# Three value projections as half-array pairs into two banks

## The chip, the cores and the metric

The kernel runs on one core of a Trainium2 chip. A core has TensorE for matrix products (PE in the profile, its weight loads PEld), VectorE (DVE) and ScalarE (ACT) for elementwise work, GpSimd (POOL) and SyncE (SP), which here mostly issue DMAs. Products land in PSUM, eight banks of 128 partitions x 512 float32; operands lie in SBUF. The metric is the device time of one execution in microseconds (us).

## The reference

Two decoder layers over 512 tokens of width 1024, float32. Each adds a token mixer and a SwiGLU to the stream, both behind an RMS norm. The second layer's mixer is windowed attention with 16 heads of 64 in three groups; the part that matters is where the values `v` come from and where they go:

```python
def attn_mixer(h, w_qkv, w_out):
    qkv = jnp.einsum('bsd,de->bse', h, w_qkv).reshape(B, S, 3, N_HEADS, HEAD_DIM)
    q = rope(qkv[:, :, 0]) * HEAD_DIM ** -0.5
    k = rope(qkv[:, :, 1])
    v = qkv[:, :, 2]
    for (window, dilation), n_g in zip(ATTN_PATTERNS, HEAD_GROUPS):   # 6, 5, 5 heads
        o_g, lse_g = dilated_window_attention(q[:, :, sl], k[:, :, sl], v[:, :, sl], window, dilation)
        ...
    alpha = jax.nn.softmax(jnp.stack(lses, axis=-1), axis=-1)
    merged = jnp.concatenate([o_g * (N_ATTN_GROUPS * alpha[:, :, g])... for g, o_g in enumerate(outs)], axis=2)
    return jnp.einsum('bse,ed->bsd', merged, w_out)
```

## The kernel before, in words

Every float32 matrix is split into a high and a low part of the type fp32r (`whi` and `wlo` for weights, `h_hi` and `h_lo` for the normed stream), and a product is three: high by high, high by low, low by high (`mm3`, lines 264 to 266). ScalarE makes the high part of a weight tile (CAST, line 171), VectorE the low one (line 175), from a raw tile that a DMA on SyncE's queue loads (line 136). Rings of five raw and five split tiles let this run ahead of TensorE: a load waits until VectorE has made the low part of the tile that lay there, a CAST until TensorE has used the split tile that lay there.

The order on TensorE is written out by hand. The orders on the other engines come from a scheduler, which plays the program through with costs of its own and puts each instruction where it is ready in that play; `tc.high_priority(URGENT)` moves an instruction ahead of others that are ready at the same time. On the chip each engine runs its list strictly in that order.

The attention layer first projects queries and keys, head pair by head pair, with `project`: 8 blocks of the inner dimension x 3 products of 128 x 512 into one bank. `later` puts scores and transposes of earlier heads between the projections; scores (line 1051) and transposes of the softmax numerators `e` (line 1086) work on the two halves of the array, 64 partitions each. Then the values come in two forms:

- The first six heads: `for m in range(3)` calls `project` for two heads at a time. ScalarE copies the bank, reordered, into `vt` (line 1258, tile `ropea`); a projection later `turn` transposes it on TensorE (line 1248), and ScalarE copies that into `v` (line 1249).
- The other ten heads in two parts of five: four banks `pv`, one for each 128 tokens; for each of four weight tiles `c` and each bank `b` six products of 128 x 320 (lines 1272 to 1274).

The banks of these steps come from one pool, `mm`, of four, handed out in turn. Two more pools of two, `psc` and `ptr`, fill the eight. A bank can be written again when the last reader of what it held before is done.

Beside it run `group_sums` and `group_weights` (called by `between` at steps 19 and 21): ScalarE takes the exponential of the heads' maxima `mx` (line 1168), VectorE reduces it into `near` (line 1173), four small DMAs on GpSimd's queue rearrange `near` over partitions into `mx` (line 1176), and VectorE copies that on (COPY, line 1181) and computes the weights of the groups from it (lines 1183 to 1208).

Of the kernel before, what the change touches and what calls it, by code (L numbers as in the profile page):

```python
# [10 lines left out]
F32 = mybir.dt.float32  # L11
# [6 lines left out]
P = 128  # L18
S = 512
D = 1024  # L20
NC = D // P
# [3 lines left out]
HD = 64  # L25
# [5 lines left out]
R = 4  # L31
# [44 lines left out]
def trunk_kernel(ctx: ExitStack, tc: tile.TileContext, x_in, xT, gam, gains, consts, ident_d, w0, wT, w1, wv, w_down, out):  # L76
# [9 lines left out]
    nc = tc.nc  # L86
# [18 lines left out]
    mm = Banks()  # L105
# [16 lines left out]
    def enqueue(src, shape, kind="w", **more):  # L122
        queue.append(dict(kind=kind, src=[src], shape=shape, **more))
        return len(queue) - 1

    def load(i):
        item = queue[i]
        shape = item["shape"]
        n = math.prod(shape)
        raw = (pools["v"] if item["kind"] == "v" else wraw).tile([P, 1024], F32, name="vraw" if item["kind"] == "v" else "wraw")  # L130
        dst = raw[:, :n]
        if len(shape) == 3:
            dst = dst.rearrange("p (g c) -> p g c", g=shape[0])
        elif item.get("rows"):
            dst = dst.rearrange("p (k c) -> p k c", k=shape[0])
        nc.sync.dma_start(dst, item["src"][0])
        for more in item["src"][1:]:
            nc.gpsimd.dma_start(dst, more, accum_op=ALU.add)  # L138
        raws[i] = raw

    def load_sums():

        done = loaded["v"]
        for i in range(len(ready), min(len(queue), len(ready) + 20)):
            if queue[i]["kind"] == "v" and "src" in queue[i] and i not in raws:
                if "v" not in pools or len(done) >= V_TILES and queue[done[-V_TILES]]["last"] >= len(ready):
                    return
                load(i)
                done.append(i)

    def weights(i, split_ahead=4, load_ahead=5, held=0):

        load_ahead = queue[i].get("ahead", load_ahead)
        for n in range(loaded["w"], min(len(queue), i + load_ahead)):
            if queue[n]["kind"] == "w":
                load(n)
            loaded["w"] = n + 1
        load_sums()
        while len(ready) < min(loaded["w"], i + split_ahead):
            item = queue[len(ready)]  # L160
            if item["kind"] == "v" and "v" not in pools:
                break
            if "pool" not in item and len(ready) > i and held + sum("pool" not in it for it in queue[i : len(ready)]) >= RING:
                break
            shape = item["shape"]
            n = math.prod(shape)
            raw = raws[item.get("into", len(ready))]
            hi, lo = (pools.get(item.get("pool"), wspl).tile([P, 1024], F32R, name=item.get("pool", "w") + part) for part in ("hi", "lo"))
            if len(ready):
                with tc.issue_after(item["cast_behind"]) if "cast_behind" in item else nullcontext():  # L170
                    nc.scalar.copy(hi[:, :n], raw[:, :n])  # L171
            else:
                nc.vector.tensor_copy(hi[:, :n], raw[:, :n])
            with tc.issue_after(item["behind"]) if "behind" in item else nullcontext():
                nc.vector.tensor_sub(lo[:, :n], raw[:, :n], hi[:, :n].bitcast(F32))  # L175
            for into, more in item.get("then", ()):
                nc.vector.tensor_add(raws[into][:, :n], raws[into][:, :n], raws[more][:, :n])  # L177
            if "loads" in item:
                into, src = item["loads"]
                nc.gpsimd.dma_start(raws[into][:, :n].rearrange("p (k c) -> p k c", k=shape[0]), src, accum_op=ALU.add)  # L180
            if len(shape) == 2:
                ready.append(tuple(t[:, :n].rearrange("p (k m) -> p k m", k=shape[0]) for t in (hi, lo)))
            else:
                ready.append(tuple(t[:, :n].rearrange("p (g k m) -> p g k m", g=shape[0], k=shape[1]) for t in (hi, lo)))
        got = ready[i]
        ready[i] = None
        return got
# [68 lines left out]
    j_v0 = [enqueue(w0[26 + i], (8, P)) for i in range(3)]  # L256
# [6 lines left out]
    def mm3(ps, whi, wlo, xhi, xlo, first, last, **kw):  # L263
        nc.tensor.matmul(ps, lhsT=whi, rhs=xhi, start=first, stop=False, **kw)  # L264
        nc.tensor.matmul(ps, lhsT=whi, rhs=xlo, start=False, stop=False, **kw)  # L265
        nc.tensor.matmul(ps, lhsT=wlo, rhs=xhi, start=False, stop=last, **kw)  # L266

    def project(j, hi, lo):
        ps = mm.tile([P, S], F32, name="mm")
        whi, wlo = weights(j)  # L270
        for k in range(NC):
            mm3(ps, whi[:, k, :], wlo[:, k, :], hi[:, k, :], lo[:, k, :], k == 0, k == NC - 1)
        return ps


    xs = stat.tile([P, 4 * D], F32, name="x")
    x = xs.rearrange("p (b d) -> p b d", b=4)
# [6 lines left out]
    def tokens_at(shift):  # L284
        both = tokens_both(shift)
        return [both[:, z] for z in range(2)]
# [17 lines left out]
    class Norm:  # L304
# [49 lines left out]
        def turn(self, b, half, tp):  # L354

            for j in range(4):
                at = half * S + j * P
                nc.tensor.transpose(tp[:, j, :], self.tile(b)[:, at : at + P], ident)
# [79 lines left out]
    with ExitStack() as pctx:  # L438
# [12 lines left out]
        h_hi, h_lo = z_hi, z_lo = tokens_at(0)  # L451
# [13 lines left out]
        for c in range(NC):  # L465

            pieces = (slice(0, P), slice(P, S)) if c == 0 else (slice(0, S),)
            if c < 2 or c % 2 == 0:
                if c < 2:
                    load_x(c, pieces[0])  # L470
                whi, wlo = weights(j_in[0][c if c < 2 else 1 + c // 2], 1, 1)
# [7 lines left out]
            k = 0 if c < 2 else c % 2  # L479
# [3 lines left out]
            for b, i in turns:  # L483
                xx, w = parts[i]
                nc.tensor.matmul(  # L485
                    early[b], lhsT=xx[:, c, b * P : (b + 1) * P], rhs=w[:, k, :],
                    start=c == 0 and i == 0, stop=c == NC - 1 and i == 2, skip_group_check=True,
# [15 lines left out]
        v, s, r = (tmp.tile([P, 4], F32, name=name) for name in ("v4", "s4", "r4"))  # L503
# [453 lines left out]
    with ExitStack() as actx:  # L957
# [20 lines left out]
        def blocks_of(a):  # L978

            return a.rearrange("p (r b i) -> p b r i", r=R, b=4)  # L980

        def rope(ps, t, name):
            a = aw.tile([P, S], F32, name="ropea")
            sw = aw.tile([P, S], F32, name="ropeb")
            nc.vector.stream_shuffle(sw, ps, PARTNER)
            nc.vector.tensor_mul(a, ps, cosr)
            nc.gpsimd.tensor_mul(sw, sw, sinr)
            out = aw.tile([P, S], F32, name=name, bufs=3)

            if t >= 3:  # L990
                nc.vector.tensor_add(out, a, sw)
            elif name == "k":
                nc.vector.tensor_add(out.rearrange("p (b r i) -> p b r i", b=4, r=R), blocks_of(a), blocks_of(sw))
            else:
                by_r = lambda z: z.rearrange("p (r j) -> p r j", r=R)
                nc.vector.tensor_add(out.rearrange("p (j r) -> p r j", r=R), by_r(a), by_r(sw))
            return out
# [116 lines left out]
        h_hi, h_lo = tokens_at(0)  # L1114
# [26 lines left out]
        for t in range(8):  # L1141
# [4 lines left out]
            k = rope(pk, t, "k")  # L1146
            later(2 * t + 1)
            if t in (4, 6):
                first = (t, q, k)
# [80 lines left out]
        def between(step, copied=None):  # L1230
            later(step)
            if step == 19:
                group_sums()
            if step == 21:
                group_weights()
            if step == 23:
                with tc.issue_after(copied.ins):
                    spread_weights()
# [11 lines left out]

        step = 16
        for m in range(3):
            ps = project(j_v0[m], h_hi, h_lo)
            if to_turn:
                turn()
            vt = aw.tile([P, S], F32, name="ropea")
            with tc.high_priority(URGENT):
                nc.scalar.copy(vt.rearrange("p (b r i) -> p b r i", b=4, r=R), blocks_of(ps))
            to_turn.append((m, vt))
            between(step)  # L1260
            step += 1
        for part in range(2):
            at = VA + part * VB
            pv = [mm.tile([P, S], F32, name="mm") for _ in range(4)]
            for c in range(4):
                whi, wlo = weights(j_v[part][c])
# [23 lines left out]
        two = mp.tile([P, D], F32, name="even_rows")  # L1290
# [110 lines left out]
```

## Time and profile before

| | us |
|---|---|
| median of three runs | 980.57 (980.44 to 980.94) |
| profiled execution | 981.05 |
| its span, first to last instruction | 979.3 |
| TensorE busy | 971.8 |
| VectorE busy | 784.1 |
| ScalarE busy | 575.9 |
| first of the three projections begins (in the span) | 542.54 |
| last of the three ends, transposes begin | 562.51 |

A row of a timeline gives the start in us from the span's beginning, the duration, engine, line, operation, output<-inputs, shape, how many, and in brackets how long the engine had been idle and who ended that. TensorE's products overlap: a product of 512 columns is listed with 0.39 us, but the next one starts 0.23 us behind it, so the cost of one is read from starts. A row of the windows view has the stretch, its length, busy time and count of PE, PEld, DVE, ACT and POOL, the clock that TensorE was granted (1.00 is full), the DMA engines' busy share, and GB/s.

### The profile page before, as it was taken

How to read it: one execution, taken by the hardware profiler on the slowest of the kernel's cores; microseconds unless marked ns; L12 is line 12 of the kernel's file. 1: busy time of each engine (PE TensorE's matmuls, PEld its weight loads, DVE VectorE, ACT ScalarE, POOL GpSimd, SP SyncE). 2: the span in 40 equal slices, each digit the busy share in tenths (PEclk: the TensorE clock that was granted, in tenths of full speed). 3: DMA queues.
4: the chain of work that ended last, by engine and by line, in shares of the span. 5: the costliest groups of instructions: out<-in, count | busy, mean ns of one | idle time of the engine just before them, and what ended most of it. 6: DMA issues, size and time to landing. Idle time of an engine off the chain costs nothing.

```text
span 979.3 us, 15534 instructions
## 1 busy us (share of the span) xinstructions
PE 971.8 (99%) x5996; PEld 863.6 (88%) x5996; DVE 784.1 (80%) x1083; ACT 575.9 (59%) x903; POOL 124.6 (13%) x124
## 2 busy tenths in 40 slices
PE   9999999999999999999999999999999999999997
PEld 8888899988988999889888898899998998899886
DVE  6475799888888888797897548579988898888876
ACT  6573566656665666574553554356664675567655
POOL 0002010011011111101211123101011001111110
PEclk9999999999999999999999999999999999999999
DMA  9548176579668877555221249627757947987752
GB/s 333 189 158 207 44 195 174 129 200 247 165 151 222 234 183 162 117 191 164 87 79 55 62 150 251 147 58 194 183 146 194 263 109 172 250 213 187 156 137 101
DMA packets 79466, 163.00 MB, mean 166 GB/s; under 512 B 6096, under 2 KB 6480, under 8 KB 79392
## 3 DMA queue, kind: packets, MB, share of 16 engines
q1 hardware_dynamic: 58544, 122.04, 38.0%
q0 software_dynamic: 20560, 39.69, 23.6%
q8 instruction: 47, 0.77, 0.3%
q14 instruction: 27, 0.22, 0.1%
q10 hardware_dynamic: 288, 0.27, 0.1%
HBM read 159.85 MB, written 2.13 MB: 165 GB/s over the span
## 4 chain that ended last, share of the span: by engine, by line
PE 99%; ACT 0%; DVE 0%; issue 0%; ACTq 0%
PE pair L674 32%; PE pair L818 21%; PE p L700 5%; PE mm L264 5%; PE mm L266 4%; PE mm L265 4%; PE pair L700 4%; PE r L700 2%; PE early L485 2%; PE mm L405 2%; PE mm L403 2%; PE mm L404 2%; PE mm L700 1%; PE mm L1272 1%; PE mm L1273 1%; PE mm L1274 1%
## 5 line engine op out<-in xcount | busy, mean ns | idle before, releaser
L175 DVE TENSOR_TENSOR wlo<-wraw,whi 128x1024 fp32r<-128x1024 f32 (+2 forms) x190 | 221.6, 1171 | 67.3 <-ACT whi L171 66.7
L171 ACT CAST whi<-wraw 128x1024 fp32r<-128x1024 f32 (+2 forms) x189 | 184.1, 979 | 138.6 <-PE pair L674 28.6
L171 ACT CAST whi<-vraw 128x1024 fp32r<-128x1024 f32 (+1 forms) x108 | 105.2, 979 | 118.5 <-DVE vraw L177 39.6
L175 DVE TENSOR_TENSOR wlo<-vraw,whi 128x1024 fp32r<-128x1024 f32 (+1 forms) x108 | 121.3, 1131 | 46.4 <-ACT whi L171 46.4
L674 PE MATMUL pair<-h,whi 128*128 128x512 f32 (+1 forms) x640 | 143.2, 349 | 0.0
L674 PEld LDWEIGHTS pair<-h,whi 128*128 128x128 f32 x640 | 109.1, 189 | 13.4
L674 PE MATMUL pair<-t,whi 128*128 128x512 f32 (+1 forms) x512 | 110.6, 337 | 0.0
L818 PE MATMUL pair<-whi,u_hi 128*128 128x512 f32 (+1 forms) x284 | 109.9, 387 | 0.0
L818 PE MATMUL pair<-wlo,u_hi 128*128 128x512 f32 (+1 forms) x284 | 109.8, 387 | 0.0
L818 PE MATMUL pair<-whi,u_lo 128*128 128x512 f32 (+1 forms) x284 | 109.7, 386 | 0.0
L674 PEld LDWEIGHTS pair<-t,whi 128*128 128x128 f32 x512 | 86.0, 190 | 8.4
L674 PE MATMUL pair<-h,wlo 128*128 128x256 f32 x512 | 89.2, 281 | 0.0
L674 PEld LDWEIGHTS pair<-h,wlo 128*128 128x128 f32 x512 | 76.1, 188 | 4.2
L138 POOL DMA_DIRECT2D wraw<-w x22 | 26.6, 1211 | 395.4 <-DMA wraw<-w 128.3
L177 DVE TENSOR_TENSOR vraw<-vraw,wraw 128x1024 f32<-128x1024 f32 (+1 forms) x66 | 75.1, 1138 | 0.7
L674 PE MATMUL pair<-t,wlo 128*128 128x256 f32 x384 | 71.9, 282 | 0.0
L264 PE MATMUL mm<-h,whi 128*128 128x512 f32 (+1 forms) x176 | 64.3, 365 | 0.0
L266 PE MATMUL mm<-h,wlo 128*128 128x512 f32 (+1 forms) x176 | 63.4, 360 | 0.0
L265 PE MATMUL mm<-h,whi 128*128 128x512 f32 (+1 forms) x176 | 63.4, 360 | 0.0
L818 PEld LDWEIGHTS pair<-whi,u_lo 128*128 128x128 f32 x284 | 53.4, 188 | 10.8
L818 PEld LDWEIGHTS pair<-whi,u_hi 128*128 128x128 f32 x284 | 53.4, 188 | 10.4
L818 PEld LDWEIGHTS pair<-wlo,u_hi 128*128 128x128 f32 x284 | 53.4, 188 | 10.2
(350 smaller groups left out, 2024.3 us busy)
## 6 DMA issues: line engine op xcount, KB each, us to landing
wraw<-w SPq DMA_DIRECT2D x116, 512.0 KB, 4.9
wraw<-w_down SPq DMA_DIRECT2D x32, 512.0 KB, 3.8
vraw<-w SPq DMA_DIRECT2D x22, 512.0 KB, 4.6
wraw<-w POOLq DMA_DIRECT2D x22, 512.0 KB, 6.8
vraw<-w POOLq DMA_DIRECT2D x22, 512.0 KB, 9.2
wraw<-wT SPq DMA_DIRECT2D x16, 512.0 KB, 4.2
vraw<-w_down POOLq DMA_DIRECT2D x12, 512.0 KB, 7.4
wraw<-w_down SPq DMA_DIRECT2D x24, 256.0 KB, 3.4
```

The costliest lines, as they stand in the source:

```text
L138: nc.gpsimd.dma_start(dst, more, accum_op=ALU.add)
L171: nc.scalar.copy(hi[:, :n], raw[:, :n])
L175: nc.vector.tensor_sub(lo[:, :n], raw[:, :n], hi[:, :n].bitcast(F32))
L177: nc.vector.tensor_add(raws[into][:, :n], raws[into][:, :n], raws[more][:, :n])
L264: nc.tensor.matmul(ps, lhsT=whi, rhs=xhi, start=first, stop=False, **kw)
L265: nc.tensor.matmul(ps, lhsT=whi, rhs=xlo, start=False, stop=False, **kw)
L266: nc.tensor.matmul(ps, lhsT=wlo, rhs=xhi, start=False, stop=last, **kw)
L403: nc.tensor.matmul(ps, lhsT=xhi, rhs=w[0][:, k, :], start=first, stop=False)
L404: nc.tensor.matmul(ps, lhsT=xhi, rhs=w[1][:, k, :], start=False, stop=False)
L674: mat = lambda o, w, m, **kw: nc.tensor.matmul(o, lhsT=w, rhs=m, skip_group_check=True, **kw)
L700: nc.tensor.matmul(ps[:, g, :], lhsT=w[:, g, c, :], rhs=right[:, z, c, :], start=i in (0, 1, 3) and g + c + k == 0, stop=c == 3 and k == 2 ...
L818: nc.tensor.matmul(acc(t), lhsT=u, rhs=w, start=first, stop=n == len(places) - 1, skip_group_check=True)
```

## The change

`project_rows` takes the place of `project` for the three value projections of the first six heads. Each product over 128 partitions becomes two over 64: the first half of the rows adds into one bank, the second half into another, and the pairs alternate. The output is the sum of the two banks: ScalarE copies the first, VectorE adds the second to the copy.

```diff
+    def project_rows(j, hi, lo):
+        two = [mm.tile([P, S], F32, name="mm") for _ in range(2)]
+        whi, wlo = weights(j)
+        for k in range(NC):
+            for w, z, first, last in ((whi, hi, k == 0, False), (whi, lo, False, False), (wlo, hi, False, k == NC - 1)):
+                for rows, ps in zip((slice(0, HD), slice(HD, P)), two):
+                    nc.tensor.matmul(ps, lhsT=w[rows, k, :], rhs=z[rows, k, :], start=first, stop=last)
+        return two
...
         for m in range(3):
-            ps = project(j_v0[m], h_hi, h_lo)
+            ps, more = project_rows(j_v0[m], h_hi, h_lo)
             if to_turn:
                 turn()
             vt = aw.tile([P, S], F32, name="ropea")
             with tc.high_priority(URGENT):
-                nc.scalar.copy(vt.rearrange("p (b r i) -> p b r i", b=4, r=R), blocks_of(ps))
+                by_block = vt.rearrange("p (b r i) -> p b r i", b=4, r=R)
+                nc.scalar.copy(by_block, blocks_of(ps))
+                nc.vector.tensor_add(by_block, by_block, blocks_of(more))
```

Line numbers behind the new function are higher by 9, behind the edit by 11 (COPY of `mx`: 1181 becomes 1190; first product into `pv`: 1272 becomes 1283). The scheduler's lists change at two places.

VectorE's list around the third projection, before. `gain<-mx` of line 1181 is the COPY that waits for the small DMAs; the two `wlo` are low parts of weights for the second part of `pv`:

```order
L1173 TENSOR_REDUCE gain_4418<-mx_4217 128x4 x2
L1195 RECIPROCAL den_4218<-den_4218 128x40
L175 TENSOR_TENSOR wlo_5515<-wraw_5460,whi_5514 128x640
L175 TENSOR_TENSOR wlo_5585<-wraw_5512,whi_5584 128x640
L1181 COPY gain_4418<-mx_4217 128x2x4
L1183 TENSOR_TENSOR gtop_5613<-gain_4418 128x4
L1184 TENSOR_TENSOR gtop_5613<-gtop_5613,gain_4418 128x4
```

The same place in the changed kernel:

```order
L1182 TENSOR_REDUCE gain_4418<-mx_4217 128x4 x2
L1204 RECIPROCAL den_4218<-den_4218 128x40
L1190 COPY gain_4418<-mx_4217 128x2x4
L1192 TENSOR_TENSOR gtop_5691<-gain_4418 128x4
L175 TENSOR_TENSOR wlo_5593<-wraw_5538,whi_5592 128x640
L1269 TENSOR_TENSOR ropea_5531<-ropea_5531,mm_5470 128x512
L1193 TENSOR_TENSOR gtop_5691<-gtop_5691,gain_4418 128x4
```

The COPY stands ahead of both `wlo` (the other one comes after the group weights) and of the third projection's add, which reads its second bank, `mm_5470`.

ScalarE's list around its copy of the third projection, before:

```order
L1007 ACTIVATE e_5380,den_4218<-e_5380,neg_5391 128x128 x2
L1258 COPY ropea_5454<-mm_5417 128x512
L1007 ACTIVATE e_5380,den_4218<-e_5380,neg_5391 128x128 x2
L1249 COPY v_4216<-sc_5448 128x4x128
L1168 ACTIVATE mx_4217<-mx_4217 128x64
L171 CAST whi_5514<-wraw_5460 128x640
L171 CAST whi_5584<-wraw_5512 128x640
```

And in the changed kernel:

```order
L1016 ACTIVATE e_5432,den_4218<-e_5432,neg_5443 128x128 x4
L1177 ACTIVATE mx_4217<-mx_4217 128x64
L171 CAST whi_5592<-wraw_5538 128x640
L1268 COPY ropea_5531<-mm_5469 128x512
L1258 COPY v_4216<-sc_5525 128x4x128
L1195 ACTIVATE gain_4418<-gain_4418 128x12
L171 CAST whi_5662<-wraw_5590 128x640
```

The copy that frees the first bank, `mm_5469`, and the copy of `v` have moved from ahead of the exponential of `mx` to behind it and behind a CAST. On TensorE the list is the same but for the products; the four banks of `pv` (numbers 5534 to 5537) are taken in turn behind the two of the third projection, so that the third of them is the bank of 5469 and the fourth that of 5470.

## The prediction

> **What bounds the kernel now.** I read the page's busy shares first, then the chain that ended last, then the list of what TensorE waited for, then the timelines of each engine around the three projections.
>
> ```profile
> PE 971.8 (99%) x5996; PEld 863.6 (88%) x5996; DVE 784.1 (80%) x1083; ACT 575.9 (59%) x903; POOL 124.6 (13%) x124
> PE 99%; ACT 0%; DVE 0%; issue 0%; ACTq 0%
> PE mm L302 <- DVE odd_rows L296: 1.1, 1, 1.1
> ```
>
> TensorE is busy for 99% of the span, it is the whole chain, and its only recorded wait is the first 1.1 us. So there are two ways to move the time: change what TensorE's own stream costs, or make TensorE wait where it never waited. A microsecond of waiting is a microsecond at the end, since no slack stands behind it.
>
> **The products.** The 24 products of one projection, on the full array:
>
> ```profile
> 542.54 0.39 PE L264 MATMUL mm<-h,whi 128*128 128x512 f32 x1
> 547.98 0.39 PE L264 MATMUL mm<-h,whi 128*128 128x512 f32 x1
> ```
>
> First product to first product of the next projection is 5.44 us, so 227 ns each. Half-array pairs stand already in the attention scores, in another data type:
>
> ```profile
> 465.40 0.38 PE L1020 MATMUL sc<-k,q 64*128 64x256 f32 x2
> 465.61 1.03 PE L1020 MATMUL mm<-k,q 64*128 64x256 f32 x8
> 1.09 4.64 PE L302 MATMUL mm<-odd_rows 128*128 128x128 f32 x20 [1.09 <-DVE odd_rows L296]
> 5.40 1.82 PE L485 MATMUL early<-whi,h 128*128 128x512 f32 x4
> 7.06 1.09 PE L485 MATMUL early<-wlo,h 128*128 128x512 f32 x4
> 7.99 1.99 PE L485 MATMUL early<-whi,h 128*128 128x512 f32 x8
> ```
>
> The two of the first row span 0.38 us together, as long as one of them lasts, so both halves run at once; in the second row eight of them last 1.03, which leaves (1.03 - 0.38) / 3 = 0.217 us from pair to pair. What would the same cost unpaired? The early full-array f32 records come every (5.40 - 1.09) / 20 = 215 ns for 128 columns, while the fp32r products beside them take (7.06 - 5.40) / 4 = 415 ns for 512, so 256 f32 columns cost about what 512 fp32r columns do. The new pairs have 512 fp32r columns, and I price a pair at 217 ns. Bounds: 216 ns (the 465.40 and 465.61 starts, 0.21) and 454 ns (two of 227 one behind the other). Middle value by the nearest row: 72 pairs x (227 - 217) = 0.7 us saved; the other end would cost 72 x 227 = 16.3 us.
>
> Going between half and full array has a price too:
>
> ```profile
> 556.93 0.50 PE L264 MATMUL mm<-h,whi 128*128 128x512 f32 x1
> 557.27 0.39 PE L265 MATMUL mm<-h,whi 128*128 128x512 f32 x1
> ```
>
> The first product behind half-array work takes 0.34 instead of 0.23, so 0.11 a switch. The change adds one ahead of the first projection, one at each of the first two transposes of values (L1248), and removes the one shown: net two, 0.2 us. TensorE's own stream thus gains 0.5 us, nothing that can be measured; about 0.2% (2 us) is what tells a change of this kernel from none.
>
> **What the second bank brings.** Each projection now needs a VectorE add behind ScalarE's copy, priced by the nearest row of that shape:
>
> ```profile
> 543.81 0.67 DVE L986 TENSOR_TENSOR ropea<-mm,angles 128x512 f32<-128x512 f32 x1
> ```
>
> Three adds, 2.0 us of VectorE. The first falls into an idle stretch. The second stands ahead of the score masks (L1061); with the projections 0.27 us earlier these want to start at 555.65 - 0.27 = 555.38, and the add can run from 554.60 to 555.25 (copy L1258 at 554.06 and wlo at 554.19, both 0.34 earlier). Covered by 0.13 us.
>
> ```profile
> 554.06 0.58 ACT L1258 COPY ropea<-mm 128x512 f32<-128x512 f32 x1
> 554.19 0.82 DVE L175 TENSOR_TENSOR wlo<-wraw,whi 128x640 fp32r<-128x640 f32 x1 [4.61 <-ACT whi L171]
> 555.65 1.29 DVE L1061 SCALAR_TENSOR_TENSOR e<-sc,gain 128x512 f32<-128x512 f32 x2 [0.64 <-PE sc L1051]
> ```
>
> The third is the matter. In the built order it stands on VectorE behind the COPY of the group maxima (L1181 of before, L1190 of the change), which waits for a DMA round trip, and ScalarE's copy of the third projection stands behind the exponential of mx and a CAST. In before both came ahead of these. The four banks are handed out in turn: of the four value products that follow, the third gets the bank that this copy frees, the fourth the bank that the add frees. TensorE runs its list in order, so it waits for both. (The wlo queued there is for the next set of value products, four weight tiles later, and isn't missed; the rest of the group weights moves with it.)
>
> When does that COPY run? Before:
>
> ```profile
> 564.12 0.56 ACT L1258 COPY ropea<-mm 128x512 f32<-128x512 f32 x1
> 564.59 0.40 ACT L1007 ACTIVATE e<-e,neg 128x128 f32<-128x128 f32 x1
> 565.37 0.57 ACT L1249 COPY v<-sc 128x512 f32<-128x512 f32 x1
> 565.84 0.26 ACT L1168 ACTIVATE mx<-mx 128x64 f32<-128x64 f32 x1
> 565.99 1.41 ACT L171 CAST whi<-wraw 128x640 fp32r<-128x640 f32 x2
> 566.37 0.20 DVE L1173 TENSOR_REDUCE near<-mx 128x4 f32<-128x24 f32 x1
> 567.29 2.25 POOL L1176 DMA_DIRECT2D mx<-near  x4 [21.95 <-ACT whi L171]
> 567.00 1.49 DVE L175 TENSOR_TENSOR wlo<-wraw,whi 128x640 fp32r<-128x640 f32 x2
> 567.78 1.09 SPq L136 DMA_DIRECT2D wraw<-wT  x2
> 570.00:571.00 1.00, 1.00 (x18) 0.81 (x19) 0.00 (x0) 0.00 (x0) 0.00 (x0) 1.00 1.04 368
> DMA to landing us min/median/max: 1.7/3.8/4.2
> 573.08 0.17 DVE L1181 COPY gain<-mx 128x8 f32<-128x8 f32 x1 [4.59 <-DMA mx<-near]
> 573.28 0.16 DVE L1183 TENSOR_TENSOR gtop<-gain 128x4 f32<-128x4 f32 x1
> ```
>
> From L1173 to L1181 it took 6.7 us: 0.9 to the first of four DMA issues, 1.7 to the last (2.25 us for four), and up to 4.2 to land, while two 512 KB weight loads, released by the two wlo above, filled the DMA engines (share 1.04, 368 GB/s). In the change the copies at 564.12 and 565.37 (0.47 each to the next row) leave the front of mx, and the chain starts 0.27 earlier: mx at 565.84 - 0.94 - 0.27 = 564.63, L1173's twin 0.53 later at 565.16, issues from 566.08 to 567.78. Both wlo now stand behind the COPY, so the second of those loads isn't released and the transfers have the engines mostly to themselves; I take the landing of 1.7 (range 1.7 to 4.2): COPY at 569.5. Then L1183's twin at 569.7, wlo 0.75 (567.00's two in 1.49), the add 0.67: bank free at 571.3.
>
> When does TensorE want it? Before:
>
> ```profile
> 562.51 0.60 PE L1248 MATMUL sc<-ident,ropea 128*128 128x128 f32 x4
> 562.87 0.39 PE L1272 MATMUL mm<-whi,h 128*128 128x320 f32 x1
> 565.59 0.31 PE L1272 MATMUL mm<-whi,h 128*128 128x320 f32 x1
> ```
>
> The fourth value product began at 565.59. In the change the third projection ends 0.5 us earlier, so the third product wants its bank at 564.2; ScalarE delivers after mx (0.15), one CAST (0.65) and the copy (0.56), at 566.0: wait 1.8 us. Six products of (565.59 - 562.87) / 18 = 0.15 later, at 566.9, the fourth wants its bank and waits until 571.3: 4.4 us. What TensorE then does at 571.3 it did at 565.6 before: **+5.7 us**. The 0.5 us saved ahead shift the whole chain and are in this sum.
>
> **The clock after the pause.** What a pause does shows at the end of the run:
>
> ```profile
> 972.57 0.28 PE L818 MATMUL pair<-whi,t 128*128 128x256 f32 x1
> 975.00:979.00 4.00, 0.00 (x0) 0.00 (x0) 0.46 (x1) 0.69 (x1) 0.00 (x0) 0.61 0.48 183
> ```
>
> The last product ends at 972.85; a mean of 0.61 over 4 us, of 1 and then 0.5, puts the fall at 975.9, 3.05 us later. The pause of 4.4 is longer. How long the slow stretch lasts shows only at the start: 415 ns per product until about 7.0, full pace behind it, 6 us from the first matmul at 1.09. At slow pace 1 - 227/415 = 45% of the time is lost: 1.4 us if it lasts 3.05, 2.7 if 6. I take 1.7, nearer to the end row, as the array here was warm until the pause; 0 stays the lower end.
>
> The Trainium skill (TensorE: Matmul & The Clock Gate, Part 1) says that a window of 3.4 us, free-running, without work halves the clock and a busy one restores it; the fall after 3.05 agrees. By that figure the loss would be 0.45 x 3.4 = 1.5 us, an estimate from that page. The Trainium skill (TensorEngine Tiling (Array Packing), Gotcha 1: PSUM Pressure) also warns that row tiles need banks of their own; no trace of before shows what that costs, and the bank here is what TensorE waits for.
>
> **Sum.** 5.7 + 1.7 = 7.4 us on the profiled execution (981.05, span 979.3, 0.05% over the median). On the median of 980.57: 988.0 us, slower by 0.75%.
>
> **Rivals.**
> - *Pause without fall of the clock.* The fall 3.05 us after the last product is one case; if it goes by fixed windows, 4.4 us can miss it. Then 980.57 + 5.7 = 986.3.
> - *Transfers as slow as before.* If the four small DMAs land in 4.2 instead of 1.7 us, the pause is 6.9: 980.6 + 8.2 + 1.4 to 2.7 = 990.2 to 991.5. For it: the median of 3.8. Against: the weight loads wait behind.
> - *The halves run one behind the other* (454 ns). The second products come 10.9 us later, the COPY at 580.9, the third projection ends at 578.9 and the fourth product starts near 582.7, against 565.6: +17.1, so 997.7. The score pairs speak against it.
> - *Not slower.* The place is the fourth product's bank. If the pool hands it a bank that is free anyway, the late COPY costs TensorE nothing and the 0.5 us saved remain: 980.1. With this hand-out it decides at the COPY: to free the bank by 566.9 it must run by 566.9 - 0.2 - 0.75 - 0.67 = 565.3, while L1173's twin begins only at 565.2 and its DMAs follow; ScalarE's 1.8 us would even then leave 981.9.
>
> **How the numbers follow.** Pause with fall 0.50, without 0.30, slow transfers 0.10, serial halves 0.05, not slower 0.05. Prediction: the first, 988.0. Range 985.5 (no fall, a pause 0.8 shorter) to 991.5 (slow transfers, long slow stretch), which leaves out the last two. Of the 0.05 not slower, 0.01 is faster by over 0.2% and 0.04 within it; slower 0.95.
>
> **What the changed profile would show.** Pairs of L282 217 ns apart, else the serial case. In the list of waits two new entries of TensorE at L1283: about 1.8 us for ropea (L1268) and 4.4 for ropea (L1269). L1190 near 569.5, the load wraw<-wT behind it, not ahead. A granted clock below 1.00 between 570 and 577, and the same rows as before behind that, 7.4 us later. I am wrong if L1283 has no such wait, or if TensorE makes the pause good later, for which no idle time of it is there.

## The result, and the profile after

The changed kernel takes 989.02 us, median of three runs (988.85 to 990.42), against 980.57 before: ratio 1.009, 95% interval 1.0067 to 1.0112. The profiled execution took 988.85 with a span of 987.1, which is 7.8 us longer than the span before. Five more runs, beside the kernel before on another chip (run e10 below), gave 988.86 against 981.05: ratio 1.0084, interval 1.0071 to 1.0098.

Busy shares and the chain that ended last, from the page of the changed kernel:

```profile
PE 973.9 (99%) x6068; PEld 864.4 (88%) x6068; DVE 786.5 (80%) x1086; ACT 576.4 (58%) x903; POOL 124.7 (13%) x124
PE 97%; ACT 1%; DVE 1%; DMA 0%; POOL 0%; issue 0%; DVEq 0%; ACTq 0%
```

TensorE is busy 2.1 us longer, and 2% of the chain now lies on ScalarE and VectorE, where before there was none. So most of the 7.8 us is waiting. What TensorE waited for:

```profile
PE mm L1283 <- DVE gtop L1193: 4.3, 1, 4.3
PE mm L1283 <- ACT ropea L1268: 1.4, 1, 1.4
```

These two are new (the 1.1 us at the start of the program is there as before). Together they are 5.7 us and stand at the first products into two of the four `pv` banks. TensorE's timeline of the changed kernel there, with the first projection's pairs ahead:

```profile
541.96 0.39 PE L266 MATMUL mm<-h,wlo 128*128 128x512 f32 x1
542.27 0.73 PE L282 MATMUL mm<-h,whi 64*128 64x512 f32 x4
542.84 0.40 PE L282 MATMUL mm<-h,wlo 64*128 64x512 f32 x2
...
547.87 0.62 PE L282 MATMUL mm<-h,whi 64*128 64x512 f32 x4
...
548.55 0.62 PE L282 MATMUL mm<-h,whi 64*128 64x512 f32 x4
...
556.38 0.66 PE L1095 MATMUL tp<-ident,e 64*128 64x64 f32 x16
...
557.39 0.40 PE L282 MATMUL mm<-h,wlo 64*128 64x512 f32 x2
...
562.17 0.39 PE L282 MATMUL mm<-h,wlo 64*128 64x512 f32 x2
562.49 0.66 PE L1257 MATMUL sc<-ident,ropea 128*128 128x128 f32 x4
562.91 0.39 PE L1283 MATMUL mm<-whi,h 128*128 128x320 f32 x1
563.13 0.31 PE L1284 MATMUL mm<-wlo,h 128*128 128x320 f32 x1
...
564.60 0.31 PE L1285 MATMUL mm<-whi,h 128*128 128x320 f32 x1
566.32 0.42 PE L1283 MATMUL mm<-whi,h 128*128 128x320 f32 x1 [1.41 <-ACT ropea L1268]
...
567.15 0.31 PE L1285 MATMUL mm<-whi,h 128*128 128x320 f32 x1
571.72 0.61 PE L1283 MATMUL mm<-whi,h 128*128 128x320 f32 x1 [4.26 <-DVE gtop L1193]
572.12 0.47 PE L1284 MATMUL mm<-wlo,h 128*128 128x320 f32 x1
572.39 0.47 PE L1285 MATMUL mm<-whi,h 128*128 128x320 f32 x1
```

A block of three pairs takes 548.55 - 547.87 = 0.68 us, 227 ns a pair: the price of a whole product. Then come the two pauses, and behind the second one the products start 0.27 us apart (572.12, 572.39), where before they stood 0.15 apart.

Where TensorE goes from whole-array to half-array work or back, time is lost: from the last whole product to the third pair it takes 542.84 - 541.96 = 0.88 us, where three whole products took 0.68, and from the last pair over the transposes of `vt` to the first value product 562.91 - 562.17 = 0.74, where it was 562.87 - 562.28 = 0.59 before. The third projection starts behind half-array transposes, and there the pairs gain: 557.39 - 556.38 = 1.01 from these transposes to the third pair, against 557.50 - 556.34 = 1.16 to the third whole product in the kernel before:

```profile
556.34 0.66 PE L1086 MATMUL tp<-ident,e 64*128 64x64 f32 x16
...
557.50 0.39 PE L266 MATMUL mm<-h,wlo 128*128 128x512 f32 x1
```

The engines that TensorE waits for, ScalarE first and VectorE below it:

```profile
564.54 0.39 ACT L1016 ACTIVATE e<-e,neg 128x128 f32<-128x128 f32 x1
...
564.93 0.24 ACT L1177 ACTIVATE mx<-mx 128x64 f32<-128x64 f32 x1
565.08 0.71 ACT L171 CAST whi<-wraw 128x640 fp32r<-128x640 f32 x1
565.69 0.58 ACT L1268 COPY ropea<-mm 128x512 f32<-128x512 f32 x1
```

```profile
565.44 0.20 DVE L1182 TENSOR_REDUCE near<-mx 128x4 f32<-128x24 f32 x1
...
569.84 0.17 DVE L1190 COPY gain<-mx 128x8 f32<-128x8 f32 x1 [3.69 <-DMA mx<-near]
...
570.15 0.83 DVE L175 TENSOR_TENSOR wlo<-wraw,whi 128x640 fp32r<-128x640 f32 x1
570.90 0.68 DVE L1269 TENSOR_TENSOR ropea<-ropea,mm 128x512 f32<-128x512 f32 x1
```

The third projection's products are over at 562.5. ScalarE reads the first bank from 565.69, behind exponentials, `mx` and a CAST; VectorE reads the second from 570.90, behind the COPY that waits 3.69 us for the small DMAs. (The list of waits names `gtop` L1193, which ran when TensorE started; the bank's reader is the add just ahead of it, and run e1 shows that it is the one.) The DMAs themselves, GpSimd's row and then their landing times:

```profile
566.36 2.25 POOL L1185 DMA_DIRECT2D mx<-near  x4 [21.35 <-ACT ropea L1268]
DMA to landing us min/median/max: 1.6/1.7/1.7
```

The clock, in the windows view (length, busy time of PE, PEld, DVE, ACT, POOL, granted clock, DMA share, GB/s):

```profile
565.00:568.00 3.00, 1.14 (x6) 0.88 (x6) 0.94 (x6) 1.75 (x5) 1.64 (x3) 1.00 0.01 0
568.00:570.00 2.00, 0.00 (x0) 0.00 (x0) 0.16 (x1) 0.00 (x0) 0.62 (x2) 0.58 0.04 2
570.00:572.00 2.00, 0.28 (x1) 0.31 (x2) 1.79 (x6) 0.11 (x1) 0.00 (x0) 0.50 0.01 4
572.00:574.00 2.00, 2.00 (x9) 1.96 (x9) 1.31 (x11) 0.36 (x2) 0.42 (x1) 0.50 0.85 272
574.00:576.00 2.00, 2.00 (x12) 2.00 (x11) 0.82 (x1) 1.06 (x2) 1.76 (x4) 0.71 0.67 232
```

If the clock goes from 1 to 0.5 and back in one step each, a mean of 0.58 over 568 to 570 puts the fall at 568.3, and 0.71 over 574 to 576 puts the rise at 575.2: 6.8 us at half pace, of which TensorE had work in the last 3.4.

The account of the 7.8 us: the fourth value product starts at 571.72 instead of 565.59, 6.13 later. What is left, 7.8 - 6.1 = 1.7, fits the slow stretch: at 0.27 us a product instead of 0.15, about 45% of its 3.4 us are lost, 1.5 us.

### The profile page after: what moved, and what is told of

It reads as the page before. It is cut to its first block, busy times and chain, and to the rows that moved or that the text cites. A ratio compares the mean times of both kernels' runs of the same rounds, so it can differ in the third digit from the quotient of the medians.

```text
span 987.1 us, 15681 instructions
## 1 busy us (share of the span) xinstructions
PE 973.9 (99%) x6068; PEld 864.4 (88%) x6068; DVE 786.5 (80%) x1086; ACT 576.4 (58%) x903; POOL 124.7 (13%) x124
## 4 chain that ended last, share of the span: by engine, by line
PE 97%; ACT 1%; DVE 1%; DMA 0%; POOL 0%; issue 0%; DVEq 0%; ACTq 0%
PE pair L683 32%; PE pair L827 21%; PE p L709 5%; PE pair L709 4%; PE mm L264 4%; PE mm L266 4%; PE mm L265 4%; PE r L709 2%; PE early L494 2%; PE mm L412 2%; PE mm L414 2%; PE mm L413 2%; PE mm L709 1%; PE mm L282 1%; PE mm L1283 1%; PE mm L1284 1%
## 5 line engine op out<-in xcount | busy, mean ns | idle before, releaser
L683 PEld LDWEIGHTS pair<-t,wlo 128*128 128x128 f32 x384 | 59.4, 190 | 2.5
L264 PE MATMUL mm<-h,whi 128*128 128x512 f32 (+1 forms) x152 | 54.8, 361 | 0.0
L266 PE MATMUL mm<-h,wlo 128*128 128x512 f32 (+1 forms) x152 | 54.1, 356 | 0.0
```

The lines of the kernel that those rows point to most:

```text
L683: mat = lambda o, w, m, **kw: nc.tensor.matmul(o, lhsT=w, rhs=m, skip_group_check=True, **kw)
```

## The experiments

**Theory.** The products cost what they cost before. The time goes to two banks that are read late, since the scheduler's lists put their readers behind other work, and to the slow clock behind the pause. **Rivals:** the half-array products, or going between half and full array, cost the time themselves; or the second bank and its adds do.

**e3: two banks and three adds, on the whole array.** Even blocks of the inner dimension go to one bank, odd ones to the other.

```diff
-            for w, z, first, last in (...):
-                for rows, ps in zip((slice(0, HD), slice(HD, P)), two):
-                    nc.tensor.matmul(ps, lhsT=w[rows, k, :], rhs=z[rows, k, :], start=first, stop=last)
+            mm3(two[k % 2], whi[:, k, :], wlo[:, k, :], hi[:, k, :], lo[:, k, :], k < 2, k >= NC - 2)
```

> Two banks and an add for each of the three projections as in the changed kernel, but 24 products on the full array, even blocks of the inner dimension into one bank and odd ones into the other. The scheduler then leaves copy, add and both low parts ahead of the COPY, as in before. Late-bank theory: 980.6, between 980.2 and 981.0, with no wait of TensorE at the value products. If two banks and an add are what costs: about 988.

Measured: 980.96 against 980.99, ratio 0.9999 (0.999 to 1.0008). ScalarE's copy of the third projection and VectorE's add, in this run's timelines:

```profile
563.62 0.56 ACT L1266 COPY ropea<-mm 128x512 f32<-128x512 f32 x1
```

```profile
564.22 0.69 DVE L1267 TENSOR_TENSOR ropea<-ropea,mm 128x512 f32<-128x512 f32 x1 [2.45 <-ACT ropea L1266]
```

Second bank and adds cost nothing here: both banks are free by 564.9, ahead of the products that want them. The copy stands ahead of three exponentials and the add ahead of the COPY of the maxima, without any edit to them. With 24 whole products these instructions keep their places but for one exponential, which in the kernel before ran ahead of the copy.

**e6 and e7: pairs in the first two projections only, and in the third only.** The others call `project` as before, without an add; `m in (0, 1)` becomes `m in (2,)` for e7.

```diff
-            ps, more = project_rows(j_v0[m], h_hi, h_lo)
+            ps, more = project_rows(j_v0[m], h_hi, h_lo) if m in (0, 1) else (project(j_v0[m], h_hi, h_lo), None)
```

> Half-array pairs, second bank and add for the first two projections alone; the third is as in before. Late-bank theory: the third's copy and both low parts stay ahead of the COPY, no wait, and 48 pairs with their switches cost 0.1 to 0.3 us: 980.8 (980.5 to 981.1). If pairs cost by themselves, two thirds of the loss are left: 986.

> The other way round: the third projection alone as pairs into two banks. Late-bank theory: all of the loss is there, 988.5 (987.8 to 989.3), with waits of about 4.3 and 1.4 us at the value products and the fall of the clock. If pairs cost by themselves, a third of the loss: 983.4.

Measured, both on one chip beside 981.13: e6 981.4, ratio 1.0004 (0.9995 to 1.0013); e7 988.88, ratio 1.008 (1.0066 to 1.0094). The third projection alone brings all of the loss, the first two none that can be told from zero. In e6 the two low parts run ahead of the COPY, as in the kernel before. So it isn't the half products as such, of which e6 has twice as many as e7.

**e1: the add ahead of the COPY.** The COPY of the group maxima is queued behind the third add on VectorE.

```diff
+            with tc.issue_after(marks["add"].ins):
                 nc.vector.tensor_copy(sums[:, :, 0, :], perm.rearrange("p r i -> p i r"))
...
+                marks["add"] = nc.vector.tensor_add(by_block, by_block, blocks_of(more))
```

> The changed kernel with one order put right: VectorE's COPY of the group maxima is queued behind the third projection's add. Late-bank theory: TensorE's wait of 4.3 us at the fourth value product goes, ScalarE's 1.4 us at the third stays, the pause is too short for the clock to fall; that product starts 1.7 to 2.0 us later than in before, so 982.3 to 982.6. If the half-array pairs or the adds themselves cost the time, the lists of VectorE change nothing: 986 or more. Side reading: with the weight load released ahead again the four small DMAs land late, near 573 as in before.

Measured: 983.42 against 980.99, ratio 1.0026 (1.0016 to 1.0036). One edit of the order takes back about 6 us, and the wait of 4.3 is gone: the fourth value product starts at 567.86, right behind the add (567.04 to 567.71) and long before `gtop` L1193's twin (571.62), which shows that the add was what TensorE waited for. The clock keeps 1.00 throughout these waits. What is left stands in TensorE's timeline of e1:

```profile
564.90 0.31 PE L1288 MATMUL mm<-whi,h 128*128 128x320 f32 x1
566.62 0.42 PE L1286 MATMUL mm<-whi,h 128*128 128x320 f32 x1 [1.41 <-ACT ropea L1271]
...
567.46 0.31 PE L1288 MATMUL mm<-whi,h 128*128 128x320 f32 x1
567.86 0.39 PE L1286 MATMUL mm<-whi,h 128*128 128x320 f32 x1
```

Start to start less the usual 0.15 these are 1.57 and 0.25 us: the copy, and the add that has to follow it. That the second one stays was not in the expectation, nor were the 0.4 us that the pairs and their neighbours cost (e9 below): the loss is 2.4 us where 1.7 to 2.0 were expected. The side reading missed too: the COPY ran at 571.03, not near 573, and the small DMAs landed within 3.2 us, beside one weight load instead of two.

**e2: also the exponential of `mx` behind ScalarE's third copy.**

```diff
+            with tc.issue_after(marks["copy"].ins):
                 nc.scalar.activation(mx, mx, AF.Exp)
...
+                marks["copy"] = nc.scalar.copy(by_block, blocks_of(ps))
```

> As e1_add_first, and ScalarE's exponential of mx is queued behind its copy of the third projection. Late-bank theory: neither wait is left, only two more switches between half and full array and pairs that cost what full products cost: 980.8, between 980.5 and 981.2. If pairs, adds or the second bank cost by themselves: 985 or more.

Measured: 983.0, ratio 1.0021 (1.0013 to 1.003), a miss by 2 us. ScalarE's timeline of e2 says why:

```profile
565.71 0.39 ACT L1016 ACTIVATE e<-e,neg 128x128 f32<-128x128 f32 x1
...
566.10 0.71 ACT L171 CAST whi<-wraw 128x640 fp32r<-128x640 f32 x1
566.71 0.57 ACT L1272 COPY ropea<-mm 128x512 f32<-128x512 f32 x1
...
567.67 0.26 ACT L1180 ACTIVATE mx<-mx 128x64 f32<-128x64 f32 x1
```

`mx` has moved behind the copy, but the copy still stands behind all sixteen exponentials and the CAST. The wait at the third value product is 1.3 us where it was 1.4 in e1, and the two intervals overlap: moving 0.15 us of work out of the copy's way is next to nothing. `mx` was the wrong suspect.

**e8: the third projection's second bank from the pool `ptr`.** The four `mm` banks are then free of the late add.

```diff
-        two = [mm.tile([P, S], F32, name="mm") for _ in range(2)]
+        two = [mm.tile([P, S], F32, name="mm"), (second or mm.tile)()]
...
+            ps, more = project_rows(j_v0[m], h_hi, h_lo, ptr_bank if m == 2 else None)
```

> The changed kernel with the third projection's second bank from another pool, so that no value product waits for the late add. The lists stay as late as they are. Late-bank theory: the 4.3 us go, ScalarE's copy now stands before the fourth product and costs 0.4 to 0.7 us: 981.2 to 981.6. If the COPY's wait on VectorE costs TensorE in another way (weights late), 985 or more.

Measured: 987.06, ratio 1.0067 (1.0054 to 1.0079): a miss by 5 us. The waits of e8, and below them its windows view:

```profile
PE tp L282 <- ACT pT L1099: 2.0, 1, 2.0
PE sc L1257 <- DVE ropea L1269: 1.3, 1, 1.3
```

```profile
557.50:559.50 2.00, 0.10 (x1) 0.00 (x0) 2.00 (x5) 0.95 (x4) 0.00 (x0) 0.98 0.21 80
559.50:561.00 1.50, 1.44 (x6) 1.17 (x8) 1.50 (x6) 1.50 (x10) 0.00 (x0) 0.50 0.04 11
561.00:562.50 1.50, 1.50 (x10) 1.21 (x8) 1.12 (x5) 1.50 (x9) 0.00 (x0) 0.50 0.00 0
562.50:564.00 1.50, 1.50 (x14) 1.18 (x14) 0.00 (x0) 1.50 (x10) 0.00 (x0) 0.89 0.00 0
```

The two waits at the value products are gone, as the theory says of banks that aren't read late. But the borrowed bank still held transposes that ScalarE had not copied out (2.0 us), the clock fell (0.5 from 559.4 to 562.8, a loss of about 0.45 x 3.4 = 1.5), and the transposes of `vt` at L1257 read the sum that the late add makes (1.3). The late add was moved from one wait to another. Counted from start to start the two waits are 2.2 and 1.5 us; with the 1.5 of the clock and some 0.4 of the pairs that is 5.6 of the 6.1. No wait for weights is in the list.

**e4: TensorE kept at work through the second pause.** Eighteen products of 128 x 512 into a spare bank, which nothing reads, stand ahead of the fourth value product.

```diff
+                    if part == 0 and c == 0 and b == 3:
+                        spare = ptr_bank()
+                        for _ in range(18):
+                            nc.tensor.matmul(spare, lhsT=whi[:, 0, :P], rhs=h_hi[:, 0, :], start=True, stop=True)
```

> The changed kernel, and ahead of the fourth value product TensorE runs 18 products of 128 x 512 that nobody reads (18 x 0.227 = 4.1 us, inside the wait of 4.3) into a bank of another pool. Late-bank theory with a clock term: the product still starts near 571.7, the granted clock stays at 1.00, and the time falls by the slow stretch, 3.44 us x 0.45 = 1.5, to 987.5 (987.1 to 988.0). If the clock cost nothing: 989.0. If TensorE's wait were not what it seems (work in its own stream), 4 us are added: 993.

Measured: 987.52 against 981.13, ratio 1.0065 (1.0053 to 1.0078), so 1.4 us less than e7 on the same chip, though e7 has only one projection as pairs; the runs of the two don't overlap. TensorE's timeline of e4:

```profile
567.64 4.27 PE L1282 MATMUL tp<-h,whi 128*128 128x512 f32 x18
572.07 0.38 PE L1287 MATMUL mm<-whi,h 128*128 128x320 f32 x1 [0.16 <-DVE gtop L1193]
572.29 0.31 PE L1288 MATMUL mm<-wlo,h 128*128 128x320 f32 x1
```

The fourth product comes as late as in the changed kernel, but it takes 0.22 to the next one instead of 0.40, and the granted clock is 1.00 throughout the stage. From the fourth value product to the end it is 986.2 - 572.07 = 414.1 us, against 415.4 in the changed kernel, 415.0 in e10 and 413.7 in the kernel before. Work that nobody reads makes the kernel faster: the clock's share is shown by itself, and it is 1.3 to 1.7 us, of which e4 takes back 0.9 to 1.3.

**e9: pairs kept, both late reads taken off the two queues.** VectorE, idle at the end of the third projection, copies both banks, and GpSimd adds the copies. **e10** is the changed kernel itself beside it.

```diff
+            with tc.issue_after(marks["copy"].ins):
                 nc.vector.tensor_mul(mx[:, 0:6, :], mx[:, 0:6, :], by_head)
                 nc.vector.tensor_mul(mx[:, 6:, :], mx[:, 6:, :], den[:, 6:, :])
...
+                else:                                           # the third projection
+                    rest = aw.tile([P, S], F32, name="ropeb")
+                    nc.vector.tensor_copy(by_block, blocks_of(ps))
+                    marks["copy"] = nc.vector.tensor_copy(rest, more)
+                    nc.gpsimd.tensor_add(by_block, by_block, blocks_of(rest))
```

> All three projections stay pairs in two banks. For the third, VectorE copies both banks at the projection's end, ahead of the products with the exponentials of the maxima (in the trace of the run that put the add first it stood idle from 562.2 to 565.5), and GpSimd adds the two copies (its nearest rows take 1.29 us). Late-bank theory: that run's 2.0 us behind the kernel before were ScalarE's copy, which its list holds behind 16 exponentials and a CAST (wait 1.41, and 0.16 until the pace is back), and the add behind it (0.25); with both banks read by 564.3 no wait of TensorE is left at the third or fourth value product, and the time is that of the kernel before plus at most 0.4: ratio 1.000 to 1.001. Rival (the pairs themselves, or going between half and full array, cost those 2 us): ratio 1.002 or more, without a wait in the list.

> The changed kernel once more, on the same chip as the run beside it, for a narrower interval: both theories 7.8 to 8.5 us over the kernel before, ratio 1.008 to 1.009; waits of 1.4 and 4.3 us at the third and fourth value product, the clock halved for 6.8 us.

Measured: e9 981.43 against 981.05, ratio 1.0005 (0.9996 to 1.0014); e10 988.86, ratio 1.0084. VectorE's timeline of e9, and GpSimd's:

```profile
562.96 0.69 DVE L1276 COPY ropea<-mm 128x512 f32<-128x512 f32 x1 [0.69 <-PE mm L282]
563.57 0.68 DVE L1277 COPY ropeb<-mm 128x512 f32<-128x512 f32 x1
```

```profile
564.33 1.29 POOL L1278 TENSOR_TENSOR ropea<-ropea,ropeb 128x512 f32<-128x512 f32 x1 [18.96 <-DVE ropeb L1277]
```

Both banks are free at 564.25, and no wait of TensorE at the value products is left. All 144 half products are still there; with e3 and e6 this rules out both rivals, but for some 0.4 us (interval up to 1.4) that pairs and their neighbours cost. In e10 the waits are 1.4 and 4.3 us again, and the clock is halved for 6.8. No version that was run was faster than the kernel before; with the pairs at 227 ns there was nothing to gain.

## Why the prediction was right

The forecast of 988.0 us, with two late banks and a fall of the clock, is what happened; 989.02 lies in its range. Step by step:

- **Price of a pair: mis-sized.** Forecast 217 ns, 0.7 us saved over 72; measured 227, nothing saved. The step took the price from score pairs of another data type, saying that 256 columns of f32 cost about what 512 of fp32r do, by rows from the start, where fp32r products of 512 columns took 415 ns each. (Its lower bound of 216 ns is a slip too: the two starts are 0.21 apart, 210 ns.) The kernel's own rows could have told: fp32r products of 512 columns take 227 ns and those of 320 take 147 (ten from 563.13 to 564.60), so 192 columns cost 80 ns, about 0.42 a column, and a straight line through the two sizes leaves some 14 ns a product that do not go with the columns. With 512 columns as before a pair had only these 14 ns to save on, and it saved none of them. That both halves run at once was right.
- **Switches: in the right places, too small.** Forecast 0.11 each, three more and one less, 0.2 us in all. Measured 0.20 at the first projection (0.88 instead of 0.68) and about 0.15 at each of the two transposes of `vt`; at the third projection's start 0.15 are gained, as forecast (1.01 instead of 1.16). The 0.11 was read off one gap, while the products on both sides lose. From the last product ahead of the first projection to the first value product it is 562.91 - 541.96 = 20.95 against 562.87 - 542.31 = 20.56 before: 0.4 longer, where 0.5 shorter was forecast. e6 (+0.3) and e9 (+0.4) agree.
- **Adds one and two hidden: right**, no wait stands there, and e6 has both.
- **Third value product: right, a little large.** Forecast 1.8, measured 1.41 (1.57 start to start). The pairs, not faster after all, ask for the bank later: 564.75 instead of 564.2.
- **COPY, landing, bank: right.** COPY forecast at 569.5, measured 569.84; the small DMAs landed in 1.6 to 1.7, as taken, where before they needed up to 4.2; the first product into the fourth bank at 571.72 against a bank free at 571.3. The 0.3 are there already at `mx` (564.93, forecast 564.63), since the projections bring no saving. The wait is 4.26 and the start-to-start loss 571.72 - 567.30 = 4.4, as forecast; the lag 6.13 against 5.7.
- **Clock: right in size, another way than argued.** Forecast 1.7, measured 1.3 to 1.7 from the fourth value product to the end (e10 and the changed kernel). But the fall came at 568.3, 0.9 us behind the end of the last product (567.46), and in e10 0.2 us behind it, not 3.05. The forecast looked at the second pause alone; the two together leave 1.15 us of work in the 3.4 us ahead of the fall. The first 6 us of the program, which it read as a slow stretch, show a granted clock of 1.00 in the windows view, so that the slow products there (415 ns) are not shown to be the clock's doing. The 45% taken from them agree with the products behind the pause (0.27 against 0.15) all the same.
- **Rivals.** Pause without fall: refuted by the granted clock and e4. Slow transfers: refuted by the landing times; no weight load was issued between the small DMAs and 571.0, in the kernel before two were. Serial halves: refuted by the pairs. Not slower: only e9, with both reads early, gets there. With the add alone in time the rival gave 981.9, 1.3 over before; e1 measured 2.4, the 0.4 of the projections and the 0.25 of the add included.
- **The sum**: 5.7 + 1.7 = 7.4 was forecast, 6.1 + 1.7 = 7.8 measured in the profiled executions (8.45 in the medians of three, 7.8 in e10). That it comes so near is in part luck. The projections are off by 0.9, 0.5 shorter against 0.4 longer; against that the third product's wait is 0.2 smaller, and the stretch ahead of the projections was 0.35 shorter in the changed kernel's trace (541.96 against 542.31). That is no part of the change: in e1, with the same instructions up to there, it was 542.26.

What the forecast took from the order of instructions, e3, e6 and e7 trace one step further back: the lists change when the third projection is issued as 48 half products instead of 24 whole ones, whatever the banks. That the scheduler reckons a half product like a whole one, and so takes the projection to end later and lets other work go first, would explain it; it is argued from this pattern and not measured.

## What to carry to other kernels

Cutting a product over 128 partitions into two that run on the halves of the array at once gained nothing here: the pair has the same 512 columns and took the same 227 ns. Look at the price per column and per product of the same data type before hoping for it. When a change alters the number of instructions on an engine that is full, compare the other engines' lists around it first: here the arithmetic was free, and the 7.8 us came from two reads that slipped behind a round trip of small DMAs. And a bank that is read late hurts wherever it goes: moved to another pool (e8) it cost 6 us, through two other waits and the clock, while reading it early on an idle engine (e9) cost nothing.

## What the runs showed of the hardware that was not expected

- **The clock falls without an idle stretch of 3.4 us, and at no fixed time behind the work.** The slow stretch lasted 3.4 us in e8, where work came back at once, and 6.8 in the changed kernel, e7 and e10, where the pause went on. In these three, with the same two pauses, the fall came 0.9, 0.3 and 0.2 us behind the end of the last product (568.3, 567.8 and 567.5). In the 3.4 us ahead of it TensorE was busy for 1.15, 1.70 and 1.75 us, and for 1.6 in e8, whose single pause was 2.0 us long. In e1, with a pause of 1.41, no stretch of 3.4 us holds less than 1.9 us of work, and the clock stayed. So the share of work seems to decide, with a bound above 1.75 of 3.4; that it lies below 1.9 holds only if the stretch that counts took in all of e1's pause, which no run shows. The Trainium skill (TensorE: Matmul & The Clock Gate, Part 1) names one idle window of about 3.4 us for the fall and a busy one for the rise: the lengths of the slow stretches agree, the idle window does not, since the 3.4 us ahead of each fall here held work.
- **The same four small DMAs took 1.6 to 1.7 us to land with the DMA engines free and up to 4.2 beside two 512 KB loads**; in e3 and e6, again beside two loads, up to 4.5 and 4.6, and in e1, with one load beside them, up to 3.2.
- **A change between whole-array and half-array work costs more than the one gap shows**: 0.15 to 0.20 us with the neighbouring products, where the gap alone had 0.11. Half-array pairs behind half-array transposes lost nothing that shows (1.01 us, and such transposes take 0.55, from 553.99 to 554.54, two pairs 0.45).
